# The feed-forward products of the latent tokens by a seven-product scheme, with the up and the down projection as two phases

## The chip, the cores and the metric

The kernel runs on one core of a Trainium2 chip. The metric is device time in microseconds, the median over runs of the whole program. Engines are named as the profile names them: PE (TensorE, matmuls; PEld is its weight loads), DVE (VectorE), ACT (ScalarE), POOL (GpSimd), SP (SyncE, which issues nearly all DMAs here). SBUF is the working memory, PSUM the eight banks in which matmuls accumulate, DRAM the memory outside.

## What is computed

A two-layer trunk over 1024 latent tokens and, in the first layer only, 256 context tokens; width 1024, feed-forward width 2816.

```python
def conv_ffn(h, w_up, conv_w, conv_b, w_down):
    u = h @ w_up                                   # 1024 -> 2 * 2816
    up = jnp.pad(u, ((0, 0), (1, 1), (0, 0)))
    u = up[:, :-2] * conv_w[0] + up[:, 1:-1] * conv_w[1] + up[:, 2:] * conv_w[2] + conv_b
    a, b = jnp.split(u, 2, axis=-1)
    return (jax.nn.silu(a) * b) @ w_down           # 2816 -> 1024

for l in range(DEPTH):                             # DEPTH = 2
    need_ctx = l < DEPTH - 1
    mx = jnp.split(silu_c @ w_mod[l] + b_mod[l], 6, axis=-1)
    ...
    yx, yc = mixing_layer(ax @ w_in[l], ac @ w_in[l], ...)
    h = h + mx[2] * (yx @ w_out[l])
    h = h + mx[5] * conv_ffn(modulate(rmsnorm(h, norm2_g[l]), mx[3], mx[4]), w_up[l], ...)
    if need_ctx:
        ...                                        # the same for the context tokens
return rmsnorm(h, final_g)
```

## The kernel before

Everything is held transposed: 128 features on the partitions, tokens along the free dimension. `PARTS` cuts the tokens into two halves of 512 latent tokens (parts 0 and 1) and the 256 context tokens (part 2).

A product in float32 precision is made of three passes in a faster format: each operand is split into a high part (rounded by a cast) and a low part (the rest), and `gemm` sums high × high, low × high and high × low in PSUM. For a weight tile of 1024 columns (`load_weights`) SP loads it into `wraw`, ACT makes `wh` (line 135) and POOL subtracts to get `wl` (line 136); for activations ACT makes `xh` and DVE or POOL makes `xl`. So each pair of 128 × 128 weights with 512 tokens costs three matmuls.

A layer runs: mixing (attention, retention, pooling), the output projection (`wo`), a norm that yields the split operands `X2` of the feed-forward stage, and then a loop over `NF` = 22 blocks `f` of 128 gate features. `up(f, ...)` makes two halves (the silu side and the linear side) of 128 features each for all tokens: 8 × 3 matmuls per half and part, into PSUM tile `u` (`uc` for the context). `conv` reads `u` from PSUM and writes the three-tap convolution `c` into SBUF (one ACT step at line 773, two DVE steps at lines 774 and 775). `gated` applies silu (line 779), multiplies by the linear side (line 780) and splits the result into `gh` and `gl`. After every second block, `down1` multiplies the last two gates with their rows of the down projection and DVE adds the result, times the modulation, into the residual `h` (line 804). The down projection of the last two blocks comes behind the loop, where the sums for the next norm are made too.

The first layer also computes the modulation columns of the second in this loop: `mods` loads a `w_mod` tile into the buffer tag that the raw weights use (`raw`, two buffers) and DVE reduces it (lines 75 and 79).

The order of each engine's instructions comes from the framework's scheduler. `plan` is the list of weight tiles in the order of use, and `prefetch` makes them two or three tiles ahead.

## Time and profile before

| | |
|---|---|
| median of 3 runs | 3109.97 us (3107.28 to 3110.94) |
| profiled execution, first to last instruction | 3108.5 us, mean granted TensorE clock 0.963 |
| PE busy | 2939.2 us (95%) |
| DVE, ACT, POOL busy | 1657.8, 968.9, 916.5 us (53%, 31%, 29%) |
| DMA | 220.20 MB, mean 71 GB/s |
| feed-forward stage of layer one, of layer two | about 783 to 1700 us, about 2338 to 3090 us |

A profile of the profiled execution has only its span, not a run's time; the span is set beside the median. A row of the groups reads: line, engine, operation, output<-inputs, shape, count | busy us, mean ns of one | idle time of the engine before them and what ended it. Matmuls overlap, so the mean duration of one is longer than the time from one to the next. In the slices each digit is a fortieth of the span; a 9 means 90% busy or more.

### The profile page before, as it was taken

How to read it: one execution, taken by the hardware profiler on the slowest of the kernel's cores; microseconds unless marked ns; L12 is line 12 of the kernel's file. 1: busy time of each engine (PE TensorE's matmuls, PEld its weight loads, DVE VectorE, ACT ScalarE, POOL GpSimd, SP SyncE). 2: the span in 40 equal slices, each digit the busy share in tenths (PEclk: the TensorE clock that was granted, in tenths of full speed). 3: DMA queues.
4: the chain of work that ended last, by engine and by line, in shares of the span. 5: the costliest groups of instructions: out<-in, count | busy, mean ns of one | idle time of the engine just before them, and what ended most of it. 6: DMA issues, size and time to landing. Idle time of an engine off the chain costs nothing.

```text
span 3108.5 us, 38118 instructions
## 1 busy us (share of the span) xinstructions
PE 2939.2 (95%) x15198; PEld 2470.5 (79%) x15198; DVE 1657.8 (53%) x2830; ACT 968.9 (31%) x1714; POOL 916.5 (29%) x522
## 2 busy tenths in 40 slices
PE   6789989989999999999999899989898999999997
PEld 4678877878788888888887788868687888888886
DVE  7886745551755555555545744564615344334345
ACT  4345542231422122222222555542223222222222
POOL 4334353323311111112211344353233222222222
PEclk8899999989999999999999999989899999999998
DMA  6343321131211222222211211221211111111111
GB/s 214 87 113 108 94 100 61 36 139 41 67 49 61 68 75 82 73 74 72 74 55 64 62 50 54 64 87 65 89 61 48 48 48 48 48 48 48 48 48 62
DMA packets 99174, 220.20 MB, mean 71 GB/s; under 512 B 42034, under 2 KB 47538, under 8 KB 98738
## 3 DMA queue, kind: packets, MB, share of 16 engines
q1 hardware_dynamic: 98708, 216.58, 22.1%
q8 instruction: 120, 1.97, 0.2%
q10 hardware_dynamic: 288, 1.18, 0.1%
q14 instruction: 58, 0.48, 0.0%
HBM read 194.64 MB, written 23.08 MB: 70 GB/s over the span
## 4 chain that ended last, share of the span: by engine, by line
PE 79%; DVE 6%; ACT 2%; POOL 1%; issue 1%; DMA 1%; SPq 0%; POOLq 0%; DVEq 0%; ACTq 0%
PE u L144 10%; PE u L145 10%; PE u L146 10%; PE dps L801 6%; PE dps L802 6%; PE dps L803 6%; PE gps L144 4%; PE gps L145 4%; PE gps L146 4%; PE ops L144 2%; PE ops L145 2%; PE ops L146 2%; PE uc L146 1%; PE uc L145 1%; PE uc L144 1%; PE pt L384 1%
## 5 line engine op out<-in xcount | busy, mean ns | idle before, releaser
L136 POOL TENSOR_TENSOR wl<-wraw,wh 128x1024 fp32r<-128x1024 f32 x182 | 455.3, 2502 | 1462.7 <-ACT wh L135 1446.7
L144 PE MATMUL u<-xh,wh 128*128 128x512 f32 x1408 | 557.3, 396 | 8.8 <-DVE c L775 6.1
L145 PE MATMUL u<-xh,wl 128*128 128x512 f32 x1408 | 556.6, 395 | 0.0
L146 PE MATMUL u<-xl,wh 128*128 128x512 f32 x1408 | 553.9, 395 | 1.5 <-DVE xl L211 1.0
L804 DVE SCALAR_TENSOR_TENSOR h<-dps,mod,h 128x512 f32<-128x512 f32 (+1 forms) x448 | 298.9, 685 | 248.5 <-PE dps L803 247.8
L144 PE MATMUL gps<-xh,wh 128*128 128x512 f32 (+1 forms) x968 | 360.8, 373 | 10.6 <-DVE kl L254 4.0
L774 DVE SCALAR_TENSOR_TENSOR c<-u,cp,c 128x1023 f32<-128x1023 f32 x88 | 112.7, 1282 | 464.4 <-ACT c L773 464.4
L145 PE MATMUL gps<-xh,wl 128*128 128x512 f32 (+1 forms) x968 | 356.0, 368 | 0.0
L146 PE MATMUL gps<-xl,wh 128*128 128x512 f32 (+1 forms) x968 | 353.7, 367 | 0.1
L801 PE MATMUL dps<-gh,wh 128*128 128x512 f32 (+1 forms) x896 | 329.6, 368 | 7.4 <-ACT gh L784 5.2
L802 PE MATMUL dps<-gh,wl 128*128 128x512 f32 (+1 forms) x896 | 330.0, 368 | 0.0
L803 PE MATMUL dps<-gl,wh 128*128 128x512 f32 (+1 forms) x896 | 326.1, 366 | 0.0
L144 PEld LDWEIGHTS u<-xh,wh 128*128 128x128 f32 x1408 | 267.1, 190 | 67.1 <-issue 6.7
L146 PEld LDWEIGHTS u<-xl,wh 128*128 128x128 f32 x1408 | 266.2, 189 | 62.3 <-DVE xl L211 3.0
L145 PEld LDWEIGHTS u<-xh,wl 128*128 128x128 f32 x1408 | 267.0, 190 | 57.7
L135 ACT CAST wh<-wraw 128x1024 fp32r<-128x1024 f32 x182 | 190.1, 1045 | 371.0 <-issue 306.7
L376 POOL TENSOR_SCALAR P<-P,rs 128x640 f32<-128x640 f32 (+2 forms) x108 | 216.7, 2018 | 239.4 <-DVE rs L371 130.2
L773 ACT ACTIVATE c<-u,cp 128x1024 f32<-128x1024 f32 x88 | 106.2, 1207 | 517.4 <-PE u L146 517.4
L144 PEld LDWEIGHTS gps<-xh,wh 128*128 128x128 f32 x968 | 186.0, 192 | 41.0 <-issue 5.6
L146 PEld LDWEIGHTS gps<-xl,wh 128*128 128x128 f32 x968 | 185.3, 192 | 27.1 <-DVE xl L211 1.1
L145 PEld LDWEIGHTS gps<-xh,wl 128*128 128x128 f32 x968 | 185.8, 192 | 25.8 <-issue 1.2
L801 PEld LDWEIGHTS dps<-gh,wh 128*128 128x128 f32 x896 | 169.9, 190 | 38.9 <-ACT gh L784 6.1
(221 smaller groups left out, 4916.0 us busy)
## 6 DMA issues: line engine op xcount, KB each, us to landing
wm<-in_w_mod_dram SPq DMA_DIRECT2D x96, 512.0 KB, 3.6
wraw<-in_w_up_dram SPq DMA_DIRECT2D x88, 512.0 KB, 3.5
wraw<-in_w_in_dram SPq DMA_DIRECT2D x46, 512.0 KB, 3.6
wraw<-in_w_down_dram SPq DMA_DIRECT2D x44, 512.0 KB, 3.5
wraw<-in_w_out_dram SPq DMA_DIRECT2D x16, 512.0 KB, 3.5
cb<-in_rpbU_dram SPq DMA_DIRECT2D x192, 40.0 KB, 2.3
r_dram<-vt SPq DMA_DIRECT2D x10, 640.0 KB, 2.9
r<-in_xT_dram SPq DMA_DIRECT2D x16, 256.0 KB, 5.7
```

The costliest lines, as they stand in the source:

```text
L135: nc.scalar.copy(wh.rearrange(flat), raw.rearrange(flat))
L136: nc.gpsimd.tensor_tensor(wl.rearrange(flat), raw.rearrange(flat), wh.rearrange(flat).bitcast(F32), op=ALU.subtract)
L144: nc.tensor.matmul(ps[:, :n], wh[:, k], xh, start=k == 0, stop=False)
L145: nc.tensor.matmul(ps[:, :n], wl[:, k], xh, start=False, stop=False)
L146: nc.tensor.matmul(ps[:, :n], wh[:, k], xl, start=False, stop=k == KT - 1)
L376: nc.gpsimd.tensor_scalar(Pb[r][:, :w], Pb[r][:, :w], rs[:, r:r + 1], None, op0=ALU.mult)
L773: nc.scalar.activation(c[:, o:o + n], s, AF.Identity, bias=bias, scale=col(1))
L774: nc.vector.scalar_tensor_tensor(c[:, o + 1:o + n], s[:, 0:n - 1], col(0), c[:, o + 1:o + n], op0=ALU.mult, op1=ALU.add)
L801: nc.tensor.matmul(ps[:, :pn], wh, gh, start=i == 0, stop=False)
L802: nc.tensor.matmul(ps[:, :pn], wl, gh, start=False, stop=False)
L803: nc.tensor.matmul(ps[:, :pn], wh, gl, start=False, stop=i == 1)
L804: nc.vector.scalar_tensor_tensor(hv(o, part), ps[:, :pn], mod[l][cd][:, 40 + o:41 + o], hv(o, part), op0=ALU.mult, op1=ALU.add)
```

## The change

For the latent tokens, both large products use Strassen's scheme in Winograd's form. The weights of one block are taken as a 2 × 2 matrix of blocks A11, A12, A21, A22 (up: silu side or linear side, by first or second half of the 1024 inputs), the tokens' operand as B11, B12, B21, B22 (first or second half of the inputs, by first or second half of the tokens). Seven products of sums replace eight: the weight sides are A11, S1 = A21 + A22, S2 = S1 − A11, A12, S3 = A11 − A21, S4 = A12 − S2, A22 (`UNITS`), the token sides B11, T1 = B12 − B11, T2 = B22 − T1, B21, T3 = B22 − B12, B22, T4 = B21 − T2. Products accumulate in three PSUM tiles a, b and c, and copies of a half-made sum are taken out on the way. Each weight side is a *unit*: 12 matmuls of 512 tokens. Context tokens keep the plain product, so in layer one the four A units carry 12 matmuls of 256 tokens as well, and a unit A21 has only these (`UNITS_C`).

- `load_unit` loads two raw tiles per block (`ura`, `urb`), makes a sum on DVE where the unit is one, the high part on ACT and the low part on POOL. `prefetch` stays four units ahead.
- `up` copies or adds the PSUM tiles into SBUF tiles `ua` and `ub`, and the convolution reads these. The gate of block f is made during block f+1 (`late`).
- `gated` writes the gate into DRAM (`g_dram`) in seven forms: the four blocks, and T1, T2, T4 made on DVE after each odd block. Context gates go to `gc_dram`.
- The down projection follows as a phase of its own: five chunks of four blocks (`NCH`), two output halves each. `fetch` stages the operands of the next chunk from DRAM through five buffers of the tag `nt` and splits them. Every product is added to the residual by DVE (`acc_h`). The last two blocks are handled as before.
- The residual is stored in `h2_dram` by `wo`, the norm is made in place in `h`, and the residual is loaded again before the down phase.
- 32 of the 48 modulation columns of layer two are computed in its own mixing stage; 16 stay in layer one's up phase.
- Between `order` and `order.close()` each engine's instructions stand in the order of the program text.

The core of the diff (removed: the old `up`, `conv`, `gated`, `down1` and their loop, printed above):

```diff
+UNITS = ("A11", "S1", "S2", "A12", "S3", "S4", "A22")
+UNITS_C = ("A11", "S1", "S2", "A12", "A21", "S3", "S4", "A22")
+PRODS = {"A11": ("B11", "a", True), "S1": ("T1", "b", True), "S2": ("T2", "a", False), "A12": ("B21", "c", True),
+         "S3": ("T3", "a", False), "S4": ("B22", "b", False), "A22": ("T4", "a", False)}
+NCH = 5
+NT = 5
...
+    def load_unit(src, i, name):
+        l, ra, rb = src
+        npl, rawx = rawpool[0]
+        if i == 0:
+            blocks.clear()
+            ta = wp.tile([128, 1024], F32, tag="raw", name="ura")
+            nc.sync.dma_start(ta, ra)
+            tb = rawx.tile([128, 1024], F32, tag="urb", name="urb", bufs=2)
+            nc.sync.dma_start(tb, rb)
+            blocks.update(A11=ta[:, :512], A12=ta[:, 512:], A21=tb[:, :512], A22=tb[:, 512:])
+        b = blocks
+        if name[0] == "S":
+            if name == "S1":
+                b["S1"], x, y, op = npl.tile([128, 512], F32, tag="nt", name="S1", bufs=NT), b["A21"], b["A22"], ALU.add
+            elif name == "S2":
+                b["S2"], x, y, op = npl.tile([128, 512], F32, tag="nt", name="S2", bufs=NT), b["S1"], b["A11"], ALU.subtract
+            elif name == "S3":
+                b["S3"], x, y, op = b["A21"], b["A11"], b["A21"], ALU.subtract
+            else:
+                b["S4"], x, y, op = b["A12"], b["A12"], b["S2"], ALU.subtract
+            nc.vector.tensor_tensor(b[name], x, y, op=op)
+        w = wp.tile([128, 2, 512], F32R, tag=("wh", "wl")[len(made) % 2], name="wu")
+        nc.scalar.copy(w[:, 0], b[name])
+        nc.gpsimd.tensor_tensor(w[:, 1], b[name], w[:, 0].bitcast(F32), op=ALU.subtract)
+        return w[:, 0], w[:, 1]
...
+            nc.sync.dma_start(h2_dram[:, o, o0:o0 + n], hv(o, part))
...
+        def pair(name, i, src, xs):
...
+            nc.scalar.copy(hi, src)
+            cnt[0] += 1
+            (nc.gpsimd if cnt[0] % 2 else nc.vector).tensor_tensor(lo, src, hi.bitcast(F32), op=ALU.subtract)
+            return hi, lo
...
+        def norm_in_place(k, part, pb):
+            v = hv(k, part)
+            nc.vector.scalar_tensor_tensor(v, v, A2[:, k:k + 1], pb, op0=ALU.mult, op1=ALU.mult)
+            if k % 2:
+                nc.scalar.activation(v, v, AF.Identity, bias=B2[:, k:k + 1])
+            else:
+                nc.vector.tensor_scalar(v, v, B2[:, k:k + 1], None, op0=ALU.add)
...
+        pb1 = sums[1].spread(psf, "a")
+        sub = lambda o, x, y: nc.vector.tensor_tensor(o, x, y, op=ALU.subtract)
+        for i in range(4):
+            norm_in_place(i, 1, pb1)
+            sub(hv(i, 0), hv(i, 1), hv(i, 0))
+            X2["T1"][i] = pair("T1", i, hv(i, 0), xs)
...
+        def product(ps, w, x, start):
+            for j, (xh, xl) in enumerate(x):
+                wh, wl = w(j)
+                for q, (lt, rt) in enumerate(((wh, xh), (wl, xh), (wh, xl))):
+                    nc.tensor.matmul(ps, lt, rt, start=start and j == 0 and q == 0, stop=j == len(x) - 1 and q == 2, skip_group_check=True)
...
+        def up(f, after):
+            ua, ub = [up_.tile([128, T], F32, tag="u", name="u", bufs=2) for _ in range(2)]
+            ps = {n: psf.tile([128, 512], F32, tag=n, name="u" + n) for n in "abc"}
+            uc = [None, None]
+            L, R = slice(0, 512), slice(512, 1024)
+            for name in (UNITS if last else UNITS_C):
+                wh, wl = [t.rearrange("p (k c) -> p k c", k=4) for t in weights()]
+                w = lambda j: (wh[:, j], wl[:, j])
+                if name != "A21":
+                    m, acc, start = PRODS[name]
+                    product(ps[acc], w, X2[m], start)
+                if name == "A11":
+                    nc.scalar.copy(ua[:, L], ps["a"])
+                elif name == "S1":
+                    nc.scalar.copy(ub[:, R], ps["b"])
+                elif name == "S2":
+                    nc.scalar.copy(ua[:, R], ps["a"])
+                elif name == "A12":
+                    nc.vector.tensor_tensor(ua[:, L], ps["c"], ua[:, L], op=ALU.add)
+                elif name == "S3":
+                    nc.vector.tensor_tensor(ub[:, R], ps["a"], ub[:, R], op=ALU.add)
+                elif name == "S4":
+                    nc.vector.tensor_tensor(ua[:, R], ps["b"], ua[:, R], op=ALU.add)
+                elif name == "A22":
+                    nc.scalar.copy(ub[:, L], ps["a"])
+                if not last and name[0] == "A":
+                    half, kh = int(name[1]) - 1, int(name[2]) - 1
+                    first = name in ("A11", "A21")
+                    if first:
+                        uc[half] = psg.tile([128, 512], F32, tag="g", name="uc")
+                    product(uc[half][:, :C], w, X2c[4 * kh:4 * kh + 4], first)
+                if name == "S2":
+                    while late:
+                        late.pop(0)()
+                if after:
+                    after(name)
+            cs = []
+            for half, u in enumerate((ua, ub)):
+                ch = f + NF * half
+                c = [up_.tile([128, T], F32, tag="c", name="c", bufs=3)]
+                if not last:
+                    c.append(up_.tile([128, C], F32, tag="cc", name="cc", bufs=2))
+                col = lambda t: cp[l][:, CP_CW + 44 * t + ch:CP_CW + 44 * t + ch + 1]
+                bias = cp[l][:, CP_CB + ch:CP_CB + ch + 1]
+                for s, d, n in zip((u, uc[half]), c, (T, C)):
+                    nc.scalar.activation(d, s[:, :n], AF.Identity, bias=bias, scale=col(1))
+                    nc.vector.scalar_tensor_tensor(d[:, 1:n], s[:, 0:n - 1], col(0), d[:, 1:n], op0=ALU.mult, op1=ALU.add)
+                    nc.vector.scalar_tensor_tensor(d[:, 0:n - 1], s[:, 1:n], col(2), d[:, 0:n - 1], op0=ALU.mult, op1=ALU.add)
+                cs.append(c)
+            late.append(lambda: gated(f, *cs))
...
+        def gated(f, ca, cb):
+            for a, b in zip(ca, cb):
+                nc.scalar.activation(a, a, AF.Silu)
+                nc.vector.tensor_tensor(a, a, b, op=ALU.mult)
+            g, p = ca[0], f // 2
+            if not last:
+                nc.sync.dma_start(gc_dram[f], ca[1])
+            if f % 2 == 0:
+                g0[0] = g
+                nc.sync.dma_start(g_dram[p][:, 0], g[:, 0:512])
+                if p == NF // 2 - 1:
+                    nc.sync.dma_start(g_dram[p][:, 1], g[:, 512:T])
+                return
+            nc.sync.dma_start(g_dram[p][:, 2:4].rearrange("p a b -> p (a b)"), g[:, 0:T])
+            if p < NF // 2 - 1:
+                ge = g0[0]
+                t1, t2, t4 = [npl.tile([128, 512], F32, tag="nt", name="gt", bufs=NT) for _ in range(3)]
+                sub(t1, ge[:, 512:T], ge[:, 0:512])
+                nc.sync.dma_start(g_dram[p][:, 4], t1)
+                sub(ge[:, 512:T], g[:, 512:T], ge[:, 512:T])
+                nc.sync.dma_start(g_dram[p][:, 1], ge[:, 512:T])
+                sub(t2, g[:, 512:T], t1)
+                nc.sync.dma_start(g_dram[p][:, 5], t2)
+                sub(t4, g[:, 0:512], t2)
+                nc.sync.dma_start(g_dram[p][:, 6], t4)
...
+        def stage(name, i, src):
+            t = npl.tile([128, 512], F32, tag="nt", name="gs", bufs=NT)
+            nc.sync.dma_start(t, src)
+            return pair(name, i, t, xs_now[0])
...
+        def fetch(ch, name):
+            G[ch, name] = [stage(name, j, g_dram[2 * ch + j][:, GPOS[name]]) for j in range(2)]
...
+        order = ExitStack()
+        order.enter_context(tc.manual_schedule())
+        for f in range(NF):
+            up(f, (lambda n: fetch(0, PRODS[n][0]) if n in ("A11", "S1", "S2", "A12") else None) if f == NF - 1 else None)
+            if l == 0 and f < 16:
+                mods(1, (f,), (0, 1), sc)
...
+        for name in ("S3", "S4", "A22"):
+            fetch(0, PRODS[name][0])
+        for k in range(KT):
+            nc.sync.dma_start(h[k], h2_dram[:, k, 0:T])
+            if not last:
+                nc.sync.dma_start(hc[k], h2_dram[:, k, T:N])
...
+        def acc_h(o, part, ps):
+            n = PARTS[part][1]
+            cd = 1 if part == 2 else 0
+            nc.vector.scalar_tensor_tensor(hv(o, part), ps[:, :n], mod[l][cd][:, 40 + o:41 + o], hv(o, part), op0=ALU.mult, op1=ALU.add)
...
+        for ch in range(NCH):
+            for half in range(2):
+                ps = {(n, q): psf.tile([128, 512], F32, tag=n, name="d" + n) for n in "abc" for q in range(2)}
+                uc = {}
+                for name in (UNITS if last else UNITS_C):
+                    wh, wl = [t.rearrange("p (k c) -> p k c", k=2) for t in weights()]
+                    for q in range(2):
+                        w = lambda j: (wh[:, j, 128 * q:128 * q + 128], wl[:, j, 128 * q:128 * q + 128])
+                        if name != "A21":
+                            m, acc, start = PRODS[name]
+                            product(ps[acc, q], w, G[ch, m], start)
+                            r, part = TARGET[name]
+                            acc_h(4 * half + 2 * r + q, part, ps[acc, q])
+                        if not last and name[0] == "A":
+                            r, kh = int(name[1]) - 1, int(name[2]) - 1
+                            first = name in ("A11", "A21")
+                            if first:
+                                uc[q] = psg.tile([128, 512], F32, tag="g", name="dc")
+                            product(uc[q][:, :C], w, [gcs[4 * ch + 2 * j + kh] for j in range(2)], first)
+                            if not first:
+                                acc_h(4 * half + 2 * r + q, 2, uc[q])
+                    if half == 1 and ch < NCH - 1 and name != "A21":
+                        fetch(ch + 1, PRODS[name][0])
+                if half == 0 and not last:
+                    for f in range(4 * ch + 4, min(4 * ch + 8, NF)):
+                        gcs[f] = ctx_g(f)
```

How the instructions stand now, at the three places that matter. SP's queue in the up phase of layer two; before, it holds weight loads alone:

```order
L124 DMA wraw<-in_w_up_dram 128x1024 x4
L124 DMA wraw<-in_w_down_dram 128x1024 x2
L124 DMA wraw<-in_w_up_dram 128x1024 x4
L124 DMA wraw<-in_w_down_dram 128x1024 x2
L124 DMA wraw<-in_w_up_dram 128x1024 x4
```

After, around an odd block (`c` is the gate, `gt` are T1, T2 and T4 of it):

```order
L920 DMA g_dram_95<-c 128x512
L140 DMA ura<-in_w_up_dram 128x1024
L142 DMA urb<-in_w_up_dram 128x1024
L924 DMA g_dram_95<-c 128x1024
L929 DMA g_dram_95<-gt 128x512
L931 DMA g_dram_95<-c 128x512
L933 DMA g_dram_95<-gt 128x512
L935 DMA g_dram_95<-gt 128x512
L140 DMA ura<-in_w_up_dram 128x1024
L142 DMA urb<-in_w_up_dram 128x1024
```

The loads of the next block's weights stand behind the stores of the gate. VectorE in the same stage, before (`h` is the residual, `c<-u` the convolution out of PSUM):

```order
L774 SCALAR_TENSOR_TENSOR c<-u,cp_73,c 128x1023
L775 SCALAR_TENSOR_TENSOR c<-u,cp_73,c 128x1023
L774 SCALAR_TENSOR_TENSOR c<-u,cp_73,c 128x1023
L804 SCALAR_TENSOR_TENSOR h_18227<-dps,mod_77,h_18227 128x512 x2
L775 SCALAR_TENSOR_TENSOR c<-u,cp_73,c 128x1023
```

And after, in an odd block (`S` sums of weights; `urb<-ura,urb` is S3, `ura<-ura,S` is S4; line 914 the gate product, line 831 the gate sums; `u<-uc`, `u<-ua` take products A12 and S3 out of PSUM):

```order
L907 SCALAR_TENSOR_TENSOR c<-u,cp_73,c 128x1023
L154 TENSOR_TENSOR urb<-ura,urb 128x512
L154 TENSOR_TENSOR ura<-ura,S_21929 128x512
L914 TENSOR_TENSOR c<-c 128x1024
L831 TENSOR_TENSOR gt<-c 128x512
L831 TENSOR_TENSOR c<-c 128x512
L831 TENSOR_TENSOR gt<-c,gt 128x512 x2
L878 TENSOR_TENSOR u<-uc,u 128x512
L880 TENSOR_TENSOR u<-ua,u 128x512
L154 TENSOR_TENSOR S_22060<-urb 128x512
```

Sums of weights, the gate's product and its sums now stand between the convolutions and the next copies out of PSUM. SP at the end of layer two's up phase (`gs` are staged operands of the down phase, `g_23450` the first residual tile), a place that the kernel before does not have:

```order
L924 DMA g_dram_97<-c 128x1024
L939 DMA gs<-g_dram_87 128x512
L939 DMA gs<-g_dram_88 128x512
L939 DMA gs<-g_dram_87 128x512
L939 DMA gs<-g_dram_88 128x512
L939 DMA gs<-g_dram_87 128x512
L939 DMA gs<-g_dram_88 128x512
L968 DMA g_23450<-h_dram 128x1024
```

The residual's loads stand behind the last gate's store and six staged operands.

260 lines of the change are left out of this document (151 added, 109 removed).

## The prediction

> **What bounds the kernel now.** I read the busy shares first, then the slices, the chain, and the costliest groups.
>
> ```profile
> span 3108.5 us, 38118 instructions
> PE 2939.2 (95%) x15198; PEld 2470.5 (79%) x15198; DVE 1657.8 (53%) x2830; ACT 968.9 (31%) x1714; POOL 916.5 (29%) x522
> PE   6789989989999999999999899989898999999997
> PEclk8899999989999999999999999989899999999998
> PE 79%; DVE 6%; ACT 2%; POOL 1%; issue 1%; DMA 1%; SPq 0%; POOLq 0%; DVEq 0%; ACTq 0%
> L144 PE MATMUL u<-xh,wh 128*128 128x512 f32 x1408 | 557.3, 396 | 8.8 <-DVE c L775 6.1
> L801 PE MATMUL dps<-gh,wh 128*128 128x512 f32 (+1 forms) x896 | 329.6, 368 | 7.4 <-ACT gh L784 5.2
> ```
>
> TensorE is busy without a break, at the full clock, in both feed-forward stages (slices 11 to 21 and 31 to 39), and 79% of the chain is its own. Its waits there are a few microseconds in all, so whatever it no longer has to do comes off the end, as long as the other engines keep up. The profiled span, 3108.5 us, lies 1.5 us under the median of the runs (3109.97). The sum is made on the span, and 1.5 is added at the end.
>
> The mean of 396 ns is not the price of a matmul, because they overlap. The rate is in the windows:
>
> ```profile
> core 0: us, PE busy (x) PEld busy (x) DVE busy (x) ACT busy (x) POOL busy (x), PEclk, DMA share, GB/s
> 250.00:450.00 200.00, 191.31 (x1145) 169.55 (x1144) 127.23 (x310) 99.13 (x258) 93.41 (x47) 0.98 0.31 95
> 1800.00:2000.00 200.00, 193.43 (x1169) 170.53 (x1168) 102.50 (x255) 105.37 (x274) 88.94 (x44) 1.00 0.20 55
> 1200.00:1250.00 50.00, 50.00 (x264) 42.60 (x263) 23.96 (x35) 8.55 (x9) 7.22 (x3) 1.00 0.21 64
> 2500.00:2550.00 50.00, 50.00 (x220) 40.92 (x219) 18.54 (x18) 12.62 (x12) 12.60 (x5) 1.00 0.17 53
> ```
>
> In the second layer all matmuls are 512 wide: 50/220 = 0.2273 us each. In the first, two of three are 512 wide and one 256 (264 in 50 us): 3 × 50/264 − 2 × 0.2273 = 0.1136 us for one of 256.
>
> **What is removed.** Up: 44 × 24 × 2 = 2112 wide matmuls a layer become 22 × 84 = 1848. Down: 20 of the 22 row blocks go from 960 to 840 (the last two stay). That is 264 + 120 a layer, 768 in all, 174.6 us if nothing else stood in the way. So a block of the up phase shrinks from 96 × 0.2273 = 21.8 us to 19.1 in layer two, and with 48 context matmuls from 27.3 to 24.5 in layer one. The question is whether VectorE, ScalarE, GpSimd and the DMA queue feed a unit of 12 matmuls (2.73 us) in time.
>
> **Prices of the new work.**
>
> ```profile
> L804 DVE SCALAR_TENSOR_TENSOR h<-dps,mod,h 128x512 f32<-128x512 f32 x344 | 255.1, 748 | 245.3 <-PE dps L803 244.9
> L75 DVE CUSTOM_DVE_ANT_0 wm<-wm,sc,cp 128x1024 f32<-128x1024 f32 x92 | 123.2, 1339 | 62.1 <-DMA wm<-in_w_mod_dram 49.1 <-issue 10.7
> L774 DVE SCALAR_TENSOR_TENSOR c<-u,cp,c 128x1023 f32<-128x1023 f32 x88 | 112.7, 1282 | 464.4 <-ACT c L773 464.4
> L79 DVE CUSTOM_DVE_ANT_0 junk<-wm,sc,mod 128x512 bf16<-128x512 f32 x60 | 49.4, 823 | 0.8
> L780 DVE TENSOR_TENSOR c<-c 128x1024 f32<-128x1024 f32 x22 | 32.9, 1497 | 0.5
> L774 DVE SCALAR_TENSOR_TENSOR c<-uc,cp,c 128x255 f32<-128x255 f32 x44 | 21.0, 476 | 16.9 <-ACT c L773 16.9
> L155 DVE TENSOR_TENSOR xl<-yna,xh 128x512 fp32r<-128x512 f32 x24 | 15.3, 685 | 0.4 <-ACT xh L154 0.3
> L500 DVE SCALAR_TENSOR_TENSOR pb<-sab,pcs,pb 64x1024 f32<-64x1024 f32 x8 | 10.2, 1281 | 0.2
> L785 DVE TENSOR_TENSOR gl<-c,gh x44: 1215/1353/1494, 840.4 to 3065.2; 128x1280 fp32r<-128x1280 f32 x22, 128x1024 fp32r<-128x1024 f32 x22
> L779 ACT ACTIVATE c<-c 128x1024 f32<-128x1024 f32 x22 | 23.4, 1062 | 39.4 <-DVE c L775 39.4
> L207 ACT CAST xh<-nt 128x512 fp32r<-128x512 f32 x18 | 11.1, 618 | 0.4
> L903 ACT ACTIVATE sc<-scb 128x512 f32<-128x512 f32 x4 | 2.4, 597 | 1.4 <-PE scb L902 1.3
> L174 POOL TENSOR_TENSOR acc<-acc,sq 128x512 f32<-128x512 f32 x24 | 31.0, 1290 | 80.2 <-ACT sq L173 79.4 <-DVE acc L174 0.9
> DMA to landing us min/median/max: 3.4/3.5/3.8
> h<-h_dram SPq DMA_DIRECT2D x8, 512.0 KB, 4.8
> cb<-in_rpbU_dram SPq DMA_DIRECT2D x192, 40.0 KB, 2.3
> 2329.43 2.39 POOL L136 TENSOR_TENSOR wl<-wraw,wh 128x1024 fp32r<-128x1024 f32 x1 [12.68 <-ACT wh L135]
> 2329.91 2.45 DVE L174 TENSOR_TENSOR acc<-acc,sq 128x512 f32<-128x512 f32 x1 [0.86 <-ACT sq L173]
> ...
> 2335.87 5.13 POOL L136 TENSOR_TENSOR wl<-wraw,wh 128x1024 fp32r<-128x1024 f32 x2 [2.34 <-DMA wraw<-in_w_up_dram]
> 2338.70 2.85 DVE L211 SCALAR_TENSOR_TENSOR xl<-nt,mod,xh 128x512 fp32r<-128x512 f32 x1
> ```
>
> So: a half-width sum or low part on DVE 0.69 us, on GpSimd 1.29; a high part on ACT 0.62, a PSUM copy 0.60; a conv step 1.28 (the same from SBUF, L500); the gate product 1.22 (the undisturbed L785 form); silu 1.06; a weight block lands 3.5 us after its issue (the first landing row is that of the weight tiles).
>
> The last four rows matter most. A sum that takes 0.69 us took 2.45: GpSimd had begun its subtraction at 2329.43, and DVE finished 0.54 after its end. The L211 form, with the conv step's operation and both inputs in SBUF, took 2.85 for the same reason and ended 0.55 after GpSimd's pair (2341.00). The L780 mean of 1.50 against 1.22 is the same thing. The conv steps before, which read PSUM, stay at 1.28. In this kernel a DVE operation with two SBUF inputs and a GpSimd operation thus take turns. The change moves the conv input from PSUM into an SBUF tile and adds weight sums, gate sums and split halves, all with two SBUF inputs. The Trainium skill, SBUF — State Buffer, section "Who interferes with whom", states this as a lock held for the whole instruction, and the trace agrees (2.45 against 0.69). Without that rule the sum would be that of the second rival below; with it, the forecast.
>
> **Up phase, layer two.** In SyncE's queue the two weight loads of block f+1 stand behind the stores of the gate of block f−1, and these wait for its product. This closes a loop, read off the queues: two loads and a store issued 1.0 (0.33 each), landing 3.5, sum S1 0.69, a low part 1.29, sum S2 0.69, two low parts 2.58, two conv steps 2.56, a low part 1.29, two conv steps 2.56, sum S3 0.69, then ScalarE in its order (high part, copy, high part, copy, silu) 3.50, product 1.22: 21.6, and 0.6 for a dozen handovers of 0.05: **22.2 us**. After an odd block come four gate sums (2.76) and a low part between (1.29) ahead of the stores: **26.3**. Mean 24.2 against 21.8 before: 22 × 2.4 = **+52 us**. TensorE would need 19.1 and waits for the rest. The 4.8 us landing of the crowded loads would make it 25.5, and no exclusion 21.9.
>
> **Up phase, layer one.** 24.5 of matmuls cover more of the loop. Counted from a block's start: A11's context product needs the bank that the context conv frees at 4.3 and waits 1.6. The convs (four of 1.28, four of 0.48 that read PSUM) end at 8.5, the modulation columns of the next layer at 11.5 (two of 0.8, one of 1.3), S3 at 12.6, ScalarE's high part, copy and silu at 15.1, the products at 16.8, in odd blocks the gate sums at 19.7, S4 20.5, its two halves 22.5, while TensorE wants S4 at 19.3. So 24.5 + 1.6 + 3.2 = 29.4 odd, 26.5 even (S4 waits 0.3), 28.0 in the 16 blocks with columns, 27.1 in the six without: 610 against 600 (22 × 27.3), **+10**.
>
> **Down phase.** In the second half of a chunk, GpSimd has 14 low parts (18.1 us) and DVE 11 two-input operations (7.6): 25.7 on the shared path against 19.1 of matmuls (VectorE's 14 adds into the residual, 0.75 from PSUM, need no turn). 6.6 come out of it, and 1.2 for VectorE's in-order wait behind staged operands (2.3 to 3.5 us to land, no row has 256 KB reads alone; I take 2.8): 7.8 for four of five chunks. Layer two: 191 + 31 = 222 against 218, **+4**. Layer one, more cover: 5 a chunk (between 2.4 by the port and 7.8): 266 against 273, **−7**.
>
> **Seams.** Start of the stage, before:
>
> ```profile
> 2334.50:2420.00 85.50, 73.08 (x288) 57.14 (x288) 12.55 (x10) 5.92 (x5) 0.92 0.14 44
> 2348.65 0.60 PE L192 MATMUL npb<-dg,ones 128*128 128x128 f32 x4
> ```
>
> 288 up matmuls where 376 fit: 20 us lost already. Now VectorE must do 38 operations behind the second half's norm (some 0.69 each, 26.5, and 7 of turns with GpSimd), starting about 10 us after the output projection ends (2334.5; the L192 row, at 2348.65, puts the second half's norm 14 behind it, with up matmuls ahead of it in the queue that the change has not there; 7 if nothing waited): block 0 ends after 46 where 19 would do, plus some half-clock matmuls (0.92 above): 29 to 31. **+10** a layer, between 0 and 20. End of the up phase: the last gate is ready 8.7 us after the last matmul, then six staged operands through five buffers (four first, two once the first are free, 6.1), the residual tile's load 3.5 to 4.8, and the first add to it. TensorE gets two units (5.5) ahead and stops, because S2 adds into the bank that this add must read: 16, and 4 for the slower clock after and for staged operands in the last block: **+20** a layer, between 8 and 26. Residual stores and gate stores ride beside other work; if they did not, they are in the +20. The 32 columns moved into layer two's mixing: the windows at 250 and 1800 show that stage with and without such work: TensorE idle 8.7 against 6.6 in 200 us, so **+4** over 350 (0 to 11).
>
> **Sum.** 52 + 10 + 4 − 7 + 20 + 40 + 4 = +123: 3108.5 + 123 + 1.5 = **3233 us**.
>
> **Rivals.** (1) The feeding keeps up: units arrive in time as in the old stage, where GpSimd rested. The steps were: −174.6 + 64 of seams and columns, **2999 us**. For it: VectorE is busy only 18.5 of 50 us at 2500. Against it: the loop. It decides if the loop takes under about 19 us, e.g. if the loads did not stand behind the stores. (2) The queues as told, but two-input operations and GpSimd overlap: layer two's loop 21.9, layer one 27.2, down 201 and 251: −40 + 64, less 4 at the start: **3130**. Against it the 2.45 row. (3) Loads land in 4.8 us since the gate's stores are in flight with them: layer two 25.5 (+81), layer one 28.5 (+28), the rest as forecast: **3280**; with each wait over 3 us at A11 bringing half-clock matmuls, up to 3340.
>
> **How the numbers follow.** Forecast 0.50 (3180 to 3275), rival one 0.15, two 0.20, three 0.15. The range 3085 to 3340 leaves out rival one and a little of both ends. A measurement here tells about 0.2% (6 us) from no change. Faster: rival one and 0.04 of rival two, 0.19; same 0.03; slower 0.78.
>
> **What would show it.** Right: windows in layer two's up phase with about 173 matmuls in 50 us (84 in 24.2) instead of 220; periods that alternate; TensorE waiting for a low part of A11 behind the load; VectorE conv steps over 1.28; a hole of 15 us or more between the phases. Wrong: 220 in 50 us there (rival one), conv steps at 1.28 (rival two), loads landing in 5 us (three).

## The result, and the profile after

| | before | after |
|---|---|---|
| median of 4 runs | 3108.62 us (3106.84 to 3110.94) | 3291.14 us (3285.74 to 3296.01) |
| profiled execution, first to last instruction | 3108.5 us | 3283.9 us |

The ratio is 1.0591 (95% interval 1.0575 to 1.0606): the change makes the kernel 182.5 us slower, though it removes 768 wide matmuls. The forecast was 3233, with a range of 3085 to 3340.

The page of the changed kernel, the lines that answer to the first ones shown of before (span, engines, TensorE by slices, shares of the chain):

```profile
span 3283.9 us, 39951 instructions
PE 2818.0 (86%) x14430; PEld 2340.4 (71%) x14430; DVE 2030.6 (62%) x3326; ACT 1260.3 (38%) x2418; POOL 1412.2 (43%) x986
PE   6889989996889899958998889989859888886886
PE 43%; DVE 21%; DMA 8%; ACT 7%; issue 6%; POOL 4%; SPq 1%; ACTq 0%; DVEq 0%; POOLq 0%
```

In slices 30 to 39, which hold layer two's feed-forward stage, one alone reads 9 for TensorE, and its share of the chain falls from 79% to 43%; VectorE and the transfers take it over. Layer two's up phase, a window of one even and one odd block, and VectorE's addition of product A12, which comes once a block (count, min/median/max ns, first and last start):

```profile
core 0: us, PE busy (x) PEld busy (x) DVE busy (x) ACT busy (x) POOL busy (x), PEclk, DMA share, GB/s
2705.00:2752.00 47.00, 40.61 (x168) 30.84 (x168) 28.23 (x29) 18.59 (x28) 21.05 (x14) 1.00 0.24 84
L878 DVE TENSOR_TENSOR u<-uc,u x21: 677/683/692, 2470.6 to 2940.8; 128x512 f32<-128x512 f32 x21
L878 DVE TENSOR_TENSOR u<-uc,u x21: 682/684/692, 838.6 to 1405.1; 128x512 f32<-128x512 f32 x21
```

There are 168 matmuls in 47 us at the full clock, so 179 in 50 (forecast 173, before 220). Twenty blocks of layer two take 470.2 us: 23.5 each, alternating between 21.5 and 25.3 (forecast 22.2 and 26.3). The last row is layer one: 28.3 each (forecast about 27.7).

The loop itself, rows of SyncE, ScalarE, GpSimd and VectorE behind an even block:

```profile
2725.90 0.33 SPq L920 DMA_DIRECT2D g_dram<-c  x1
2726.32 0.38 SPq L140 DMA_DIRECT2D ura<-in_w_up_dram  x1
2726.80 0.40 SPq L142 DMA_DIRECT2D urb<-in_w_up_dram  x1
2730.34 0.62 ACT L156 CAST wu<-ura 128x512 fp32r<-128x512 f32 x1 [5.23 <-DMA ura<-in_w_up_dram]
2731.04 1.29 POOL L157 TENSOR_TENSOR wu<-ura,wu 128x512 fp32r<-128x512 f32 x1 [4.01 <-ACT wu L156]
2731.51 1.37 DVE L154 TENSOR_TENSOR S<-urb 128x512 f32<-128x512 f32 x1 [4.04 <-DMA urb<-in_w_up_dram]
```

The gate's store goes out at 2725.90, the next block's weights directly behind it; ScalarE then sits idle for 5.2 us and VectorE for 4.0 until they land. The sum S took 1.37 us instead of 0.69, because GpSimd's low part was running. The loop's members are those of the prediction.

The boundary between the phases, TensorE's rows in layer one and in layer two, and the tail, ScalarE's rows:

```profile
1485.68 0.58 PE L858 MATMUL dc<-gc,wu 128*128 128x256 f32 x1 [33.91 <-ACT gc L981]
3005.34 1.22 PE L858 MATMUL da<-ph,wu 128*128 128x512 f32 x2 [17.45 <-DVE g L975]
3240.83 0.63 ACT L216 ACTIVATE sq<-g 128x512 f32<-128x512 f32 x1 [1.11 <-POOL acc L217]
3251.26 0.59 ACT L1091 COPY pbs<-npb 128x512 f32<-128x512 f32 x1 [9.80 <-PE npb L235]
3251.74 0.42 ACT L212 ACTIVATE acc<-g 128x256 f32<-128x256 f32 x1
```

Layer one's hole is twice layer two's: it waits for the context gates, whose loads stand behind all the residual's. In the tail ScalarE waits 9.8 us for a copy of the first part's norm, and the next part's squares (L212) stand behind it. From the start of the last matmul of the down projection to the end of VectorE's last operation it takes 30.8 us, 16.4 before.

### The profile page after: what moved, and what is told of

It reads as the page before. It is cut to its first block, busy times and chain, and to the rows that moved or that the text cites. A ratio compares the mean times of both kernels' runs of the same rounds, so it can differ in the third digit from the quotient of the medians.

```text
span 3283.9 us, 39951 instructions
## 1 busy us (share of the span) xinstructions
PE 2818.0 (86%) x14430; PEld 2340.4 (71%) x14430; DVE 2030.6 (62%) x3326; ACT 1260.3 (38%) x2418; POOL 1412.2 (43%) x986
## 3 DMA queue, kind: packets, MB, share of 16 engines
q1 hardware_dynamic: 153860, 319.89, 29.5%
## 4 chain that ended last, share of the span: by engine, by line
PE 43%; DVE 21%; DMA 8%; ACT 7%; issue 6%; POOL 4%; SPq 1%; ACTq 0%; DVEq 0%; POOLq 0%
PE da L858 5%; DMA urb<-in_w_up_dram 4%; PE ua L858 4%; DVE c L906 4%; PE gps L187 3%; PE gps L188 3%; PE gps L189 3%; PE dc L858 3%; PE uc L858 3%; PE ub L858 3%; PE db L858 2%; DVE c L907 2%; PE ops L187 2%; PE ops L188 2%; PE ops L189 2%
## 5 line engine op out<-in xcount | busy, mean ns | idle before, releaser
L858 PE MATMUL ua<-ph,wu 128*128 128x512 f32 x1408 | 456.4, 405 | 103.0 <-ACT u L872 61.7
L157 POOL TENSOR_TENSOR wu<-ura,wu 128x512 fp32r<-128x512 f32 x192 | 264.6, 1378 | 414.1 <-ACT wu L156 382.9
L858 PEld LDWEIGHTS ua<-ph,wu 128*128 128x128 f32 x1408 | 263.0, 192 | 184.4 <-ACT u L872 71.7
L187 PE MATMUL gps<-xh,wh 128*128 128x512 f32 (+1 forms) x968 | 360.7, 373 | 22.4 <-ACT vt L262 12.1
L157 POOL TENSOR_TENSOR wu<-urb,wu 128x512 fp32r<-128x512 f32 x160 | 221.8, 1386 | 289.0 <-ACT wu L156 282.7
L858 PE MATMUL ua<-pl,wu 128*128 128x512 f32 x704 | 280.0, 398 | 0.0
L858 PE MATMUL ub<-ph,wu 128*128 128x512 f32 x704 | 235.3, 413 | 25.1 <-ACT ph L794 16.3
L858 PE MATMUL da<-ph,wu 128*128 128x512 f32 x640 | 208.6, 408 | 44.2 <-ACT wu L156 26.7
L157 POOL TENSOR_TENSOR wu<-S,wu 128x512 fp32r<-128x512 f32 x128 | 174.0, 1370 | 143.7 <-ACT wu L156 142.4
L179 POOL TENSOR_TENSOR wl<-wraw,wh 128x1024 fp32r<-128x1024 f32 x54 | 133.7, 2476 | 237.0 <-ACT wh L178 225.2
L906 DVE SCALAR_TENSOR_TENSOR c<-u,cp,c 128x1023 f32<-128x1023 f32 x88 | 138.7, 1576 | 112.9 <-ACT c L905 112.9
L858 PEld LDWEIGHTS ub<-ph,wu 128*128 128x128 f32 x704 | 137.4, 198 | 64.7 <-ACT ph L794 16.9
L858 PEld LDWEIGHTS da<-ph,wu 128*128 128x128 f32 x640 | 122.5, 197 | 71.5 <-ACT wu L156 29.4
```

The costliest lines, as they stand in the source:

```text
L157: nc.gpsimd.tensor_tensor(w[:, 1], b[name], w[:, 0].bitcast(F32), op=ALU.subtract)
L179: nc.gpsimd.tensor_tensor(wl.rearrange(flat), raw.rearrange(flat), wh.rearrange(flat).bitcast(F32), op=ALU.subtract)
L187: nc.tensor.matmul(ps[:, :n], wh[:, k], xh, start=k == 0, stop=False)
L858: nc.tensor.matmul(ps, lt, rt, start=start and j == 0 and q == 0, stop=j == len(x) - 1 and q == 2, skip_group_check=True)
L906: nc.vector.scalar_tensor_tensor(d[:, 1:n], s[:, 0:n - 1], col(0), d[:, 1:n], op0=ALU.mult, op1=ALU.add)
```

## The experiments

Each kernel is the changed one with the edit shown, of which the core is printed (`...` stands for lines left out); times are medians, ratios are to the kernel before. Stage times come from each kernel's profiled execution.

**Loads ahead of the stores (layer two).**

```diff
+                if name == "A11" and (last):
+                    nxt = next(j for j in range(len(made), len(plan)) if plan[j][1][2] == "A11")
+                    ahead.append(load_raw(*plan[nxt][0][1:]))
```

> The weight loads of block f+1 of layer two's up phase are issued at the start of block f, ahead of the stores of the gate of block f-1; layer one and all computing as they were. Theory A (the loop through the load queue sets layer two's period, 23.5 us in the trace of the changed kernel, where GpSimd and VectorE sit idle 4 to 9 us a block for the load): the loop is cut, and the period falls to the next bound, 19.5 us of work on the shared path of GpSimd and VectorE, with some waits 20 to 21: about -65 us, 3225. Theory B (the taking of turns between VectorE and GpSimd sets the period, and the wait for the load is only where the slack shows): nothing gained on the load, 23 or more, 3280 to 3291. Theory C (landing in a crowded queue): the loads still land late, but 20 us ahead of need: as A.

3241.87 us, ratio 1.0432 (1.0417 to 1.0448): 49 us gained. The addition of A12, blocks 0 to 20 of layer two:

```profile
L886 DVE TENSOR_TENSOR u<-uc,u x21: 675/681/690, 2479.5 to 2903.1; 128x512 f32<-128x512 f32 x21
PE ua L863 <- DVE u L888: 22.4, 9, 2.5
```

21.2 us a block instead of 23.5: the loop through SyncE's queue was the bound. It ended 0.2 above the expected 20 to 21. What is left is not the load: in every second block TensorE waits 2.5 us for an addition (L888) that stands behind the gate sums on VectorE. From one addition of A12 to the next such a block takes 24.1; timed on TensorE, from the first matmul of one S1 product to that of the next, it takes 22.0 to 23.7, and the others 19.3.

**Low parts on VectorE, loads where they were.**

```diff
-        nc.gpsimd.tensor_tensor(w[:, 1], b[name], w[:, 0].bitcast(F32), op=ALU.subtract)
+        (nc.vector if in_up[0] else nc.gpsimd).tensor_tensor(w[:, 1], b[name], w[:, 0].bitcast(F32), op=ALU.subtract)
```

> The low part of each weight unit of both up phases is made on VectorE instead of GpSimd; the loads stand where they stood. Theory A (loop): the loop holds four to five low parts, each 1.29 on GpSimd and 0.69 on VectorE, so layer two's period falls from 21.5 and 25.4 to about 19.2 and 22.5, layer one's from 28.5 to about 27; convolution steps all at 1.28 us, no VectorE operation of two inputs over its undisturbed time: about -85 us, 3205. Theory B (port): with GpSimd silent the turns are gone, and the period falls to VectorE's own work, 17.4 us a block, covered by 19.1 of matmuls: layer two at 19.5, layer one at 25: -160 us, 3130. Rival D (no turns are taken, and VectorE merely gets 4.8 us a block more to do): 3291 to 3390.

3388.53 us, ratio 1.0905 (1.0888 to 1.0921): slower by 97. The convolution steps of layer two, in the changed kernel (first row, L906) and here (second row, L907 is the same step), then three waits here (total us, times, longest):

```profile
L906 DVE SCALAR_TENSOR_TENSOR c<-u,cp,c x40: 1283/1786/2320, 2480.5 to 2928.5; 128x1023 f32<-128x1023 f32 x40
```

```profile
L907 DVE SCALAR_TENSOR_TENSOR c<-u,cp,c x38: 1275/1281/1286, 2519.5 to 2997.7; 128x1023 f32<-128x1023 f32 x38
...
DVE wu L158 <- ACT wu L157: 132.6, 94, 5.0
ACT wu L157 <- DMA ura<-in_w_up_dram: 123.2, 18, 8.9
PE ua L859 <- DVE u L881: 82.3, 18, 6.6
```

The turns are real: with GpSimd silent every step takes 1.28, with it up to 2.32. Yet theories A and B both fail on the time, and rival D has the time but not the reason, since its premise (no turns) is refuted. By the waits, what decides is VectorE's queue. A low part has to wait for ScalarE's high part (132.6 us in all), the first one of a block for the load too, and the additions out of PSUM stand behind it, so TensorE waits 82.3 us for L881. On GpSimd only the next low parts stood behind that wait, and TensorE waited 7.6 us for them in the changed kernel. Layer two's blocks take 26.2 us, layer one's 29.7. The Trainium skill, Perfetto Trace Analysis, section "Tensor Engine Instruction (MATMUL, LD_WEIGHTS)", says that VectorE, ScalarE and GpSimd take their instructions strictly in order; these waits agree with it.

**Both edits.** 

> Both edits: layer two's weight loads ahead of the stores, low parts of the up phases on VectorE. Theory A: no loop and no turns in layer two, the matmuls (19.1) bound it: period 19.3 to 20; layer one as with the low parts alone, 27: 3291 - 85 - 35 = 3170. If VectorE's order of work is a bound of its own: layer two at 21, 3200.

3277.12 us, ratio 1.0546 (1.0531 to 1.0562).

```profile
L887 DVE TENSOR_TENSOR u<-uc,u x21: 679/682/692, 2512.9 to 2937.1; 128x512 f32<-128x512 f32 x21
```

Layer two stands at 21.2 a block, the case "VectorE's order is a bound of its own". With the loads out of the way the wait behind L881 shrinks (TensorE's waits for that addition come to 14.3 us, 82.3 in the run before), and GpSimd's silence leaves the mean as it was: 21.2 with turns, 21.2 without. The equal means hide two changes, though: timed on TensorE, the blocks with gate sums fell from about 22.8 to 21.7 us and the others rose from 19.3 to 20.4. The run thus does not show that the turns cost nothing: part of what it saves on them may go into the low parts on VectorE. Layer one, whose loads stayed behind the stores, stays at 29.8.

**Loads ahead in both layers.** Layer one has no second buffer while the modulation columns use the same tag, so its 16 columns move to its mixing stage.

```diff
-            if l == 0 and f < 16:
-                mods(1, (f,), (0, 1), sc)
...
+                if l == 0:
+                    mods(1, list(range(16))[h * 16 // 6:(h + 1) * 16 // 6], (0, 1), sc)
...
-                if name == "A11" and (last):
+                if name == "A11" and (True):
```

> Weight loads ahead of the gate stores in both up phases. To free a second buffer for them in layer one, its 16 modulation columns go from the up phase to layer one's mixing stage (its blocks without columns took 27.4 us in the trace of the changed kernel). Theory A (the loop through the load queue also sets layer one's period of 28.6): layer one falls to the matmuls' 24.5 and some, 25; layer two as measured, 21.2; the moved columns cost 10 to 15 in mixing: 3291 - 79 - 49 + 12 = 3175. Rival (layer one is set by the order of VectorE's and ScalarE's work, not by the loads): 27.4, as without columns: 3228.

3227.83 us, ratio 1.0386 (1.0371 to 1.0402), the rival's figure. The additions of A12 in layer one, then two stretches of layer one, each from the first matmul of an S1 product to that of the next, and TensorE's wait for the bank of the context product in the changed kernel and here:

```profile
L887 DVE TENSOR_TENSOR u<-uc,u x21: 683/685/692, 858.0 to 1394.4; 128x512 f32<-128x512 f32 x21
902.80:929.50 26.70, 25.41 (x134) 21.38 (x133) 16.84 (x22) 11.35 (x18) 10.68 (x8) 1.00 0.30 104
929.50:956.10 26.60, 25.32 (x134) 21.50 (x133) 13.07 (x18) 11.43 (x18) 10.26 (x8) 1.00 0.17 55
```

```profile
PE uc L858 <- DVE cc L907: 41.1, 19, 3.9
```

```profile
PE uc L864 <- DVE cc L916: 24.3, 19, 1.3
```

Layer one takes 26.8 a block by its additions, which come 24.0 and 29.2 apart by turns, because the gate sums push back every second one. TensorE itself takes 26.6 to 26.7 in every block, where it took 26.6 to 28.4 and 28.1 to 30.3 by turns; 24.5 of it is matmuls, and 1.3 the wait for the bank that VectorE's context convolution frees. The rival's total is met in part by luck: the blocks fell below its 27.4, and the moved columns cost some 18 us of mixing, more than expected. Since loads and columns move in one edit, the run does not tell what each is worth; the last six blocks of the changed kernel, which have no columns, took 27.4.

**Another order in the up phase**, on top of that: the silu side's convolution ahead of unit A22, the gate sums behind the additions.

```diff
+                if name == "A22":
+                    conv(0)
...
+                if name == "S3":
+                    while late2:
+                        late2.pop(0)()
```

> As the run with loads ahead in both layers, and within a block of the up phase VectorE's and ScalarE's work stands in another order: the silu side's convolution ahead of the last unit instead of behind it, the gate sums behind the additions of A12 and S3 instead of ahead of them. Theory (with the loads out of the way, in-order waits behind convolution and gate sums hold the odd blocks at 24.1): layer two's period falls from 21.2 to the shared path's 19.5 to 20, layer one by 0 to 0.5: 35 below the run with loads ahead in both. Rival (the shared path of VectorE and GpSimd alone sets it, and its waits remain in any order): within 8 of that run.

3178.33 us, ratio 1.0224 (1.0206 to 1.0243): 50 below the run before.

```profile
L905 DVE TENSOR_TENSOR u<-uc,u x21: 677/678/692, 2451.6 to 2841.0; 128x512 f32<-128x512 f32 x21
2600.00:2639.00 39.00, 38.91 (x170) 31.48 (x169) 28.08 (x29) 18.58 (x28) 20.00 (x15) 1.00 0.29 101
```

Layer two's blocks take 19.5, with TensorE busy 38.91 of 39 us; layer one's 25.9, where 24.5 is matmuls. Layer two's up phase is bound by matmuls again. The turns are still there; layer two's period lies near both the matmuls' 19.1 and the shared path's 19.5, and no run separates the two.

**The boundary, first try: residual and context gates first.**

```diff
-        for name in ("S3", "S4", "A22"):
-            fetch(0, PRODS[name][0])
-        for k in range(KT):
...
+        load_h(0)
+        load_h(1)
+        gcs = {} if last else {f: ctx_g(f) for f in range(4)}
+        load_h(2)
+        load_h(3)
+        for name in ("S3", "S4", "A22"):
+            fetch(0, PRODS[name][0])
```

> At the start of the down phase the first residual tiles and layer one's context gates are loaded ahead of the six staged operands and of the other residual tiles. If the queue order makes the hole between the phases (33.9 us of TensorE idle ahead of the first context product in layer one, 17.5 us behind the first addition in layer two): layer one's hole falls to about 18, layer two's to about 11: -22 us, 3269. If the holes wait for memory that the last gate frees, or for that gate itself, the loads can't start sooner: within 5 us of 3291.

3282.70 us, ratio 1.0560 (1.0543 to 1.0578). TensorE's waits at the boundary, layer one, then layer two:

```profile
PE dc L858 <- ACT gc L969: 16.7, 1, 16.7
PE da L858 <- DVE g L991: 4.1, 1, 4.1
...
PE da L858 <- DVE g L991: 20.3, 1, 20.3
```

Layer one's hole fell from 33.9 to 16.7 and 4.1 as told. Layer two's grew from 17.5 to 20.3: the tile was there, but VectorE's three low parts of staged operands (the other three are GpSimd's) stood ahead of the addition, and the first of them waited 10.9 us for ScalarE's high part.

**The boundary, second try: the staged operands behind the first units.**

```diff
+                    if ch == half == 0 and name in ("A11", "S1", "S2"):
+                        fetch(0, PRODS[{"A11": "S3", "S1": "S4", "S2": "A22"}[name]][0])
```

> As the run with the residual first, and the last six staged operands are loaded and split behind the units A11, S1 and S2 of the first chunk instead of ahead of it. In that run the first residual tile had landed, but VectorE's six low parts of staged operands stood ahead of the first addition in its queue (hole of 20.3 us in layer two, 16.7 and 4.1 in layer one). Theory (head of VectorE's queue): layer two's hole falls to about 9 to 11, layer one's to 13 in all, if no new wait comes behind: -18, 3265. Rival (memory freed by the last gate): as that run, 3283.

3291.05 us, ratio 1.0586 (1.0567 to 1.0605): nothing gained on the changed kernel.

```profile
2989.41 1.22 PE L858 MATMUL da<-ph,wu 128*128 128x512 f32 x2 [9.22 <-DVE g L989]
3007.09 1.19 PE L858 MATMUL da<-ph,wu 128*128 128x512 f32 x2 [9.76 <-ACT wu L156]
3000.13 1.18 DVE L796 TENSOR_TENSOR pl<-gs,ph 128x512 fp32r<-128x512 f32 x1 [9.13 <-ACT ph L794]
```

The hole in layer two fell to 9.2 as expected, and 18 us later a new one of 9.8 opened: VectorE stood 9.1 us at the low part of a staged operand (third row), with sums of weights and additions behind it. The wait had only moved. Layer one's holes were 16.8 and 7.0, where 13 in all was expected.

**The tail: more buffers.** Squares, normalised tiles and copies take the tag of idle staged operands.

```diff
-            sq = self.pool.tile([128, self.n], F32, tag="nt", name="sq", bufs=NT)
+            sq = pool.tile([128, self.n], F32, tag=tag, name="sq", bufs=nb)
...
+            x.sqt = (xs2, "x2", 14)
```

> In the tail of each feed-forward stage the squares of the norm sums, the normalised tiles and the copies of the last norm get the 14 idle buffers of the staged operands instead of the five shared ones, of which three hold sums and two the copies. Theory (scarce buffers): in the changed kernel the last matmul of layer two lies 33 us ahead of the end, before 20, because one square at a time alternates with one addition; and the first 60 us of layer two's mixing lose 15: both go, -25, 3266. Rival (VectorE's order: the scaling of the output stands ahead of the last sums): no change, 3291.

3300.51 us, ratio 1.0623 (1.0607 to 1.0639): the theory of scarce buffers fell. Layer two's tail stayed at 30.8, and layer one's end became 6 us longer. The start of layer two's mixing gained nothing either: from the last matmul of layer one's down projection to the end of layer two's output projection it took 638.5 us, in the changed kernel 633.7.

**Staged operands spread over both halves**, on top of the reordered kernel, each loaded one unit ahead of its split (`LOAD` and `SPLIT` name the unit for each).

```diff
-                    if half == 1 and ch < NCH - 1 and name != "A21":
-                        fetch(ch + 1, PRODS[name][0])
+                    if ch < NCH - 1:
+                        if (half, name) in SPLIT:
+                            fetch_split(ch + 1, SPLIT[half, name])
+                        if (half, name) in LOAD:
+                            fetch_load(ch + 1, LOAD[half, name])
```

> As the run with the other order in the up phase, and the staged operands of the next chunk of the down phase are split over both halves of a chunk (four in the first, three in the second, before all seven in the second), each loaded one unit ahead of its split. Theory (the shared path in second halves: 14 low parts on GpSimd and 11 two-input operations on VectorE, 25.7 us against 19.1 of matmuls, plus VectorE's in-order wait for the landing): a chunk falls from 45 to about 40, layer two's down phase by 25, layer one's by 10 to 15: 3178 - 38 = 3140. Rival (the wait at a chunk's start, 5.5 us for the high part of a weight unit behind its load, comes from the load queue alone and stays): within 8 of 3178.

3183.66 us, ratio 1.0253 (1.0236 to 1.0270): within the rival's 8. From its first to its last addition out of PSUM tile a (`g<-da`), layer two's down phase grew from 225.0 to 234.5; layer one's fell from 275.5 to 272.2. Layer two's growth lies in the first half of the first chunk, which took 29.3 us instead of 18.7 (from the first addition of an A11 product to that of the next half). SyncE's queue:

```profile
2959.12 38.51 SPq L961 DMA_DIRECT2D gs<-g_dram  x12
2997.68 0.43 SPq L139 DMA_DIRECT2D ura<-in_w_down_dram  x1
```

Twelve loads of staged operands held the queue for 38.5 us, each waiting for one of five buffers, and the next weights stood behind them.

**Four seams**, on top of that.

```diff
-            (nc.gpsimd if cnt[0] % 2 else nc.vector).tensor_tensor(lo, src, hi.bitcast(F32), op=ALU.subtract)
+            (nc.gpsimd if rawpool[0] and cnt[0] % 2 else nc.vector).tensor_tensor(lo, src, hi.bitcast(F32), op=ALU.subtract)
...
+            up(f, first_chunk if f == NF - 1 else None)
...
+            load_h((0, 1))
+            gcs = {f: ctx_g(f) for f in range(4)}
...
+                for p in done[-1:]:
+                    nc.scalar.copy(pbs[p], sums[p].spread(psf, "c")[:, :PARTS[p][1]])
```

> As the run with the staged operands spread, and four seams: (1) low parts of the token operands at a stage's start on VectorE alone (theory of turns: VectorE's sums there take 1.75 us instead of 0.69, -4 a layer; rival, VectorE has the more to do: +4); (2) in the last block of the up phase the staged operands are loaded one unit ahead of their split (-6 a layer if VectorE's queue stands behind a landing load there); (3) layer one's context gates and two residual tiles ahead of the staged operands (-10, as measured alone); (4) in layer two's tail the copy of a part's norm stands behind the next part's sums on ScalarE, not ahead of them (the tail of 30.8 back to about 17, -14; rival: unchanged). Together 44 below the run with the operands spread, about 3096.

3156.90 us, ratio 1.0165 (1.0150 to 1.0180): 27 gained of 44. VectorE's sums at layer two's start, in the changed kernel and here:

```profile
L831 DVE TENSOR_TENSOR h<-h,h x12: 679/1218/1759, 2440.2 to 2460.2; 128x512 f32<-128x512 f32 x12
```

```profile
L840 DVE TENSOR_TENSOR h<-h,h x12: 696/702/711, 2399.2 to 2414.8; 128x512 f32<-128x512 f32 x12
```

Without GpSimd beside them they take 0.70, and each stage starts 3.5 to 4 us earlier: here the turns had a price. The last block lost 5 to 6 us less a layer, but layer two's first addition then came 4.8 later behind it. The tail fell from 30.8 to 22.5, so the order on ScalarE was 8 of the 14 us. The context gates gave 1 us net, where 10 were expected: the boundary kept the rest in other waits.

**Weights ahead of the staged operands in the down phase**, the operands in the second half again.

```diff
+                    if name == "A11" and (ch, half) != (NCH - 1, 1):
+                        nxt = next(j for j in range(len(made), len(plan)) if plan[j][1][2] == "A11")
+                        ahead.append(load_raw(*plan[nxt][0][1:]))
```

> As the run with four seams, with the staged operands again in the second half of each chunk as in the changed kernel, and the weight loads of the next half of the down phase issued at the start of a half, ahead of the staged operands' loads. In the run with the operands spread, SyncE stood 35 us at loads of staged operands that waited for one of five buffers, with weight loads behind them. Theory (this queue, not the shared path alone, holds the down phase): the 5.5 us waits at the start of each chunk go, layer two's down phase falls from 225 to about 205, layer one's by about 10: about 3157 - 40 = 3117. Rival (the shared path of 25.7 us in second halves): 225 stays, and only the 10 of the spreading come back in layer two: 3145 to 3150.

3142.70 us, ratio 1.0116 (1.0100 to 1.0133). TensorE's waits in layer two's down phase, in the changed kernel and here:

```profile
PE da L858 <- ACT wu L156: 22.6, 5, 5.5
```

```profile
PE da L866 <- ACT wu L163: 22.2, 5, 5.4
```

Layer two's down phase took 225.0 again, as with the loads behind: the rival's figure held. Freeing the queue does nothing there, and the wait of 5.4 per chunk is the same, so the load queue is not what holds the down phase. One such wait in the changed kernel, rows of VectorE, ScalarE and TensorE:

```profile
3043.23 1.74 DVE L154 TENSOR_TENSOR S<-S,ura 128x512 f32<-128x512 f32 x1
3044.90 1.40 DVE L975 SCALAR_TENSOR_TENSOR g<-da,mod,g 128x512 f32<-128x512 f32 x2
3045.09 0.62 ACT L156 CAST wu<-S 128x512 fp32r<-128x512 f32 x1 [2.63 <-DVE S L154]
3045.78 1.19 PE L858 MATMUL da<-ph,wu 128*128 128x512 f32 x2 [5.50 <-ACT wu L156]
```

Two things end just ahead of TensorE's start: the first of VectorE's two additions out of tile a, which the next product writes, and ScalarE's high part of S2. Both stand behind the sum S2 on VectorE (first row), which took 1.74 us. The wait thus comes through VectorE's order; whether the shared path as a whole (25.7 us in second halves) sets it is what the next run asks.

**The same with the operands spread again.** 

> As the run before it, with the staged operands spread over both halves again. Theory (the queue had spoiled the spreading): with the weights' loads ahead of it, the shared path has 19.7 and 17.7 us in the two halves against 19.1 of matmuls, and layer two's down phase falls to about 200, layer one's by 5: 3107. Rival (five buffers are too few for operands one unit ahead, in any order of the queue): as or above the run before it.

3149.40 us, ratio 1.0141 (1.0122 to 1.0160), the rival: layer two's down phase took 233.1. The chunks themselves did not change: from one second half to the next they took 46.6, 45.6 and 46.5 us, in the run before 46.5, 45.5 and 46.5, now split 22 and 24 instead of 26 and 20. The first half of the first chunk alone grew, from 18.8 to 31.2. So balancing the shared path to 19.7 and 17.7 us did not bring a chunk near the 38.2 of its matmuls, and the sum of that path is not shown to hold it. TensorE waited ten times (28.2 us) instead of five; what holds a chunk at 46 is not settled.

None of these versions beats the kernel before. In the best (3142.70) the two feed-forward stages take as long as before within 3 us each: of the 175 us of matmuls saved some 130 are spent at starts, boundaries, down phases and tail, and some 40 in the up blocks, most of them layer one's. The 29 us that remain on the spans lie in the mixing stages.

## Why the prediction was right

Terms in us against before, on the spans. Matmul time before is 480 and 240 us (up and down) in layer two, 600 and 300 in layer one; what its stages took beyond that, 34 and 42 with the tail apart, is counted as its start. Blocks are timed by the additions of A12, the down phase by the first and last additions out of PSUM tile a and the last plain matmul.

| term | predicted | measured |
|---|---|---|
| layer two: up blocks | +52 | +37 (22 × 1.7) |
| start | +10 | +11 |
| boundary | +20 | +25 (last block 9, hole and wait 15) |
| down | +4 | +11 |
| tail | none | +14 (30.8 against 16.4) |
| layer one: up blocks | +10 | +23 (22 × 1.05) |
| start | +10 | +2 |
| boundary | +20 | +24 |
| down | −7 | +8 |
| hand-over and mixing of layer two | +4 | +25 |
| mixing of layer one | none | −5 |
| sum | +123 | +175 |

**How near the time came, and why.** The measured 3291 lies inside the range, but above the forecast's own band (3180 to 3275) and nearest to rival three's 3280, whose late loads were to make layer two's blocks 25.5 us; they took 23.5. The direction and the loop were earned; that the range reached as far as 3291 was luck, since its upper end had been set for that other mechanism. The sum was 52 us short: layer two's blocks were priced 15 too high, the other terms together 67 too low.

**The loop held.** It was read off the queues before any run, was within 0.7 us a block, and cutting it alone gave 2.3 us a block. One step went otherwise: TensorE was to wait for a low part of A11 behind the load, but its waits are mostly for ScalarE's copies (L872) and VectorE's additions (L880), which stand behind the convolutions in order; the load had made those late.

```profile
PE ua L858 <- ACT u L872: 31.5, 19, 1.8
PE ua L858 <- DVE u L880: 13.6, 9, 1.5
PE ua L858 <- POOL wu L157: 7.6, 9, 0.9
```

**The turns are right as a fact and were overrated as a bound.** The step "no exclusion: layer two's loop 21.9" priced them at 2.3 us a block. Taking GpSimd away with the loads ahead left the mean where it was (21.2 both, from two changes that cancel), and the better order reached 19.5 with the turns in place, so they do not hold a block above that. They counted at the stage's start. What removing them alone would give in the original order was not tried free of the low parts' in-order waits.

**Rival one** (feeding keeps up) was wrong for the kernel as written and right for the mechanism it named: with loads ahead of the stores, and another order, the up blocks are fed in time. It was wrong even then on the total, since 3178 is not 2999: the seams are larger than its 64. **Rival three** half happened: the weights landed in 3.8 and 4.5 us (before 3.5), and the odd blocks were still under the forecast.

```profile
ura<-in_w_up_dram SPq DMA_DIRECT2D x20, 512.0 KB, 3.8
urb<-in_w_up_dram SPq DMA_DIRECT2D x20, 512.0 KB, 4.5
```

**What failed.** First, "Residual stores and gate stores ride beside other work; if they did not, they are in the +20" and the sum as a whole left the end of a stage out: 14 us in layer two's tail, and some 13 at the start of layer two's mixing, where TensorE has two long waits (12.1 and 7.0 us), one of them ahead of the spread of a later part's norm. ScalarE's order explains 8 of the 14; the rest, and the mixing start, are open. The columns in the mixing stage may be under-priced too: the sum had 4 us for 32 of them in layer two, and 16 moved into layer one's mixing cost 18. No run moved the 32 back.

Second, "layer one, more cover: 5 a chunk" stands in a down phase that came out 15 us off, but the chunks are not the reason: from one second half to the next they took 52.7 to 52.8 us, 3.6 to 3.7 over their matmuls. The first half took 40.9, since the hole for the context gates reaches 12.7 us into it; the boundary term had not counted these gates, which stood behind sixteen residual loads. In layer two the 7.8 a chunk was right in size (45.7 to 46.9 us against 38.2) and not in its make-up: a wait of 5.5, 1.7 to 2.9 us lost to slower matmuls behind it, and halves that do not follow the sum of the shared path when it is balanced.

Third, "28.0 in the 16 blocks with columns" was too low for the even blocks, not the odd ones: by the additions, odd blocks took 29.5 (forecast 29.4) and even ones 27.4 (forecast 26.5). The sum had A11's context product wait 1.6 for the bank that the context convolution frees, and a wait of 3.2 for S4 in odd blocks. The first was there and larger, 41.1 us in 19 blocks. Of the second, TensorE's matmuls show no more than 3.7 us in 8 blocks, for a low part ahead of a product into tile b.

One reading of the lines was off without weight in the sum: slice 31 of before reads 8, not 9; it is the start of the stage, whose lost 20 us the seams count.
